# Two thirds of the modulation in 16 steps of 256 columns on four column tiles, not 32 steps of 512 columns on two

## The chip, the cores and the metric

The kernel runs on one core of a Trainium2 chip. The metric is the device time of one execution in microseconds; less is better. Times of before are the median of three runs, and the profile is of one execution.

## The reference

One decoder layer, for a prompt group of 1024 tokens and a sample group of 8 sequences with one new token each. Of it the change touches the modulation: a vector per sequence (8 of the sample group and one of the prompt, so 9) goes through `silu`, a matrix of 1024 x 6144 and a bias, and gives shift, scale and gate for the two halves of the layer.

```
mod = (jax.nn.silu(c) @ w_ada + b_ada)[:, None, :]
shift1, scale1, gate1, shift2, scale2, gate2 = jnp.split(mod, 6, axis=-1)
h = x * (1 + scale1) + shift1
qa, ka, va, rq, rk, rv, rg, ga, gb = jnp.split(h @ w_in, _in_splits(), axis=-1)
...
y_att = o_att.reshape(B, S, ATTN_OUT_WIDTH) @ w_att_out
y_ret = (jax.nn.silu(rg) * o_ret) @ w_ret_out
mixed = (jax.nn.sigmoid(ga) * y_att + jax.nn.sigmoid(gb) * y_ret) @ w_o
x = _layer_norm(DEEPNORM_ALPHA * x + gate1 * mixed, ln1_g, ln1_b)
h2 = x * (1 + scale2) + shift2
```

Only shift1 and scale1 (the first third, columns 0 to 2047) are needed before the input projection; gate1, shift2, scale2 and gate2 (the last two thirds) are first needed after `w_o`.

## The kernel before

Activations lie transposed in on-chip slots, 128 features by 1032 tokens each. A large product is done by `dense`: for one block of 128 output columns it goes over three chunks of 384, 384 and 264 tokens, and in each chunk `mm3` issues three matmuls for every block of 128 inputs (value and remainder: high x high, high x low, low x high), lines 191 to 193, into one bank `ps_d`. With 8 input blocks a dense is 72 matmuls, with 2 it is 18. Weights come through `wload`: a DMA from the SP queue into `w_raw` (line 174), a cast to `w_hi` on ScalarE (line 154) and a subtraction to `w_lo` on VectorE (line 155), each in a ring of three buffers, so a weight is cast when the dense three before it has ended.

The first third of the modulation is made at the start, by `prep`, eight times: 256 columns, all eight input blocks, in two loads of four blocks. The last two thirds are made by the generator `ada_rest`, which is advanced inside the loops over the gates. The gate loop A has eight rounds: a dense of 8 blocks for `ga` (called GA here) with a sigmoid on ScalarE as its evacuation (line 813), then a dense of 2 blocks for the attention output (called ATT) with a multiplication on VectorE (line 816). The gate loop G has eight rounds of one dense of 8 blocks (GB, sigmoid at line 827).

A matmul of the modulation (line 224, `ada_mm`) has the 9 vectors, padded to 32, as its stationary operand `cs`. Input block k writes the 32 PSUM partitions of column tile k modulo 4, and the four partial sums are added afterwards: `ada_finish` copies the bank to `m` on ScalarE (line 208), transposes it by blocks of 128 columns on TensorE (line 211), sums the four partial sums with a reduction on VectorE (line 214) and adds the bias (line 218). The loads `ada_raw` (line 232) and the copies `m` take slots from a first-in, first-out list of 40; in the last round of loop A 36 of them are held (16 by `hT`, 8 by `gated`, 4 by `oa`, 8 by `A`), and 4 go round.

Instructions stand on each engine in the order that the framework's scheduler gives them, so a transpose can stand some matmuls behind the step that it belongs to. An engine takes its instructions in that order.

Of the kernel before, what the change touches and what calls it, by code (L numbers as in the profile page):

```python
# [33 lines left out]
C_QA, C_KA, C_VA, C_RQ, C_RK, C_RV, C_RG, C_GA, C_GB = (  # L34
    0, 768, 1536, 2304, 2816, 3328, 4352, 5376, 6400)
# [69 lines left out]
def tile_hybrid_decoder_step(ctx: ExitStack, tc: tile.TileContext, a, o):  # L105
    nc = tc.nc
    dma_w = nc.sync
# [9 lines left out]
    slots = Slots()  # L117
    slots.add(slot_pool, N_SLOTS, "s")

    def bank(tag, shape, bufs):  # L120
        full = psum.tile([128, 512], F32, tag=tag, name="ps_" + tag, bufs=bufs)
        rows, inner = shape[0], shape[1:]
        n = int(np.prod(inner))
        ap = full[:rows, :n]
        if len(inner) == 2:
            ap = ap.rearrange("p (a b) -> p a b", a=inner[0])
        elif len(inner) == 3:
            ap = ap.rearrange("p (a b c) -> p a b c", a=inner[0], b=inner[1])
        return ap

    def dbank(shape=(128, 512)):
        return bank("d", shape, 3)

    def abank(shape=(128, 512)):
        return bank("a", shape, 2)

    def bbank(shape=(128, 512)):
        return bank("b", shape, 2)
# [33 lines left out]
    def wload(src, shape, eng=nc.vector, with_raw=False):  # L172
        raw = stream.tile(list(shape), F32, tag="raw", name="w_raw")
        dma_w.dma_start(raw[:], src)
        hi = stream.tile(list(shape), F32R, tag="hi", name="w_hi")
        lo = stream.tile(list(shape), F32R, tag="lo", name="w_lo")
        split(raw[:], hi[:], lo[:], eng)
        if rolling[0]:
            roll(hi)
        return (hi, lo, raw) if with_raw else (hi, lo)  # L180

    def wcols(w, c0, nk=8, k0=0, eng=nc.vector):
        return wload(w[128 * k0:128 * (k0 + nk), c0:c0 + 128].rearrange("(k p) c -> p k c", p=128),
                     (128, nk, 128), eng)

    def mm3(ps, w, acts, t0, n, k0=0, first=True, last=True):
        whi, wlo = w
        nk = len(acts)
        for k, (xhi, xlo) in enumerate(acts):
            f, l = first and k == 0, last and k == nk - 1  # L190
            nc.tensor.matmul(ps, whi[:, k0 + k, :], xhi[:, t0:t0 + n], start=f, stop=False)  # L191
            nc.tensor.matmul(ps, whi[:, k0 + k, :], xlo[:, t0:t0 + n], start=False, stop=False)  # L192
            nc.tensor.matmul(ps, wlo[:, k0 + k, :], xhi[:, t0:t0 + n], start=False, stop=l)  # L193

    def dense(w, acts, evac, chunks=TCH, k0=0, between=None):
        for t0, n in chunks:
            ps = dbank((128, n))
            mm3(ps, w, acts, t0, n, k0)
            evac(t0, n, ps)
            if between:  # L200
                next(between, None)

    w_ada, w_in = a["w_ada"], a["w_in"]

    def ada_finish(ps, chunks):
        n = 128 * len(chunks)
        m = slots.alloc((128, n), name="m")
        nc.scalar.copy(m[:], ps)
        pt = bbank((128, len(chunks), 128))
        for j, c in enumerate(chunks):  # L210
            nc.tensor.transpose(pt[:, j, :], m[:, 128 * j:128 * j + 128], ident[:])
        for j, c in enumerate(chunks):
            parts = pt[:, j, :].rearrange("p (g r) -> p r g", g=4)
            nc.vector.tensor_reduce(modT[:, c, :], parts[:, 0:9, :], axis=AX.X, op=OP.add)
        c0, n = chunks[0], len(chunks)
        step = chunks[1] - c0
        mt = modT[:, c0:c0 + (n - 1) * step + 1:step, :]
        nc.vector.tensor_add(mt, mt, bT[:, c0:c0 + (n - 1) * step + 1:step].unsqueeze(2).to_broadcast([128, n, 9]))
        slots.free(m)

    def ada_mm(ps, k0, w):
        for k in range(w.shape[1]):
            g = (k0 + k) % 4
            nc.tensor.matmul(ps[32 * g:32 * g + 32], cs[:, k0 + k, :], w[:, k],  # L224
                             start=k0 + k < 4, stop=k0 + k >= 4)

    def ada_rest():
        for cg in range(4, 12):
            ps = abank((128, 512))
            for k0 in range(0, 8, 2):  # L230
                raw = slots.alloc((128, 2, 512), name="ada_raw")
                dma_w.dma_start(raw[:], w_ada[128 * k0:128 * k0 + 256, 512 * cg:512 * cg + 512]
                                .rearrange("(k p) c -> p k c", p=128))
                ada_mm(ps, k0, raw)
                slots.free(raw)
                if k0 == 6:
                    ada_finish(ps, range(4 * cg, 4 * cg + 4))
                yield

    rc, rs = slots.alloc(name="rope_c"), slots.alloc(name="rope_s")  # L240
    for t, v, r in ((rc, 1.0, 0), (rs, 0.0, 1)):
# [34 lines left out]
    hT = []  # L276
# [95 lines left out]
    for g, (win, dil) in enumerate(PATTERNS):  # L372
        ls = min(dil, 8)
        qk = []
        for c0 in (C_QA, C_KA):
            for p in range(2):
                dst = slots.alloc(name="qk")

                def evac(t0, n, ps, dst=dst):
                    sh = wk.tile([128, 384], F32, tag="sh", name="sh", bufs=2)  # L380
                    t1 = wk.tile([128, 384], F32, tag="t1", name="t1", bufs=2)
                    nc.vector.stream_shuffle(sh[:, :n], ps, shuf)
                    nc.vector.tensor_mul(t1[:, :n], ps, rc[:, t0:t0 + n])
                    nc.vector.tensor_mul(sh[:, :n], sh[:, :n], rs[:, t0:t0 + n])
                    m = min(n, S - t0)
                    if dil == 1:
                        nc.vector.tensor_add(dst[:, t0:t0 + n], t1[:, :n], sh[:, :n])
                    else:
                        ov = dst[:, :S].rearrange("p (r u) -> p u r", r=ls)[:, t0 // ls:(t0 + m) // ls, :]
                        nc.vector.tensor_add(ov, t1[:, :m].rearrange("p (u r) -> p u r", r=ls),  # L390
                                             sh[:, :m].rearrange("p (u r) -> p u r", r=ls))
                        if n > m:
                            nc.vector.tensor_add(dst[:, S:T], t1[:, m:n], sh[:, m:n])

                if g == 0 and c0 == C_QA:
                    for (t0, n), ps in zip(TCH, first_ps[p]):
                        evac(t0, n, ps)
                else:
                    dense(wcols(w_in, c0 + 256 * g + 128 * p), hT, evac)
                qk.append(dst)  # L400
# [29 lines left out]
        for bi in range(8):  # L430
# [6 lines left out]
            nk, k0 = 128 * len(kb), 128 * kb[0]  # L437
# [228 lines left out]
    for h in range(4):  # L666
# [3 lines left out]
        for c0 in (C_RQ, C_RK):  # L670
            dst = slots.alloc(name="rqk")

            def evac(t0, n, ps, dst=dst):
                sw = wk.tile([128, 384], F32, tag="sh", name="sw", bufs=2)
                t1 = wk.tile([128, 384], F32, tag="t1", name="t1", bufs=2)
                nc.scalar.copy(sw[0:64, :n], ps[64:128])
                nc.scalar.copy(sw[64:128, :n], ps[0:64])
                nc.vector.tensor_mul(t1[:, :n], ps, rc[:, t0:t0 + n])
                nc.vector.tensor_mul(sw[:, :n], sw[:, :n], rs[:, t0:t0 + n])
                nc.vector.tensor_add(dst[:, t0:t0 + n], t1[:, :n], sw[:, :n])  # L680

            dense(wcols(w_in, c0 + 128 * h), hT, evac)
            qk.append(dst)
# [117 lines left out]
    oa = []  # L801
    for p in range(2):
# [3 lines left out]
        oa.append((hi, lo))  # L806
    A, G = [], []
    ada = ada_rest()
    for f in range(8):
        A.append(slots.alloc(name="A"))  # L810

        def sig(t0, n, ps, dst=A[f]):
            nc.scalar.activation(dst[:, t0:t0 + n], ps, AF.Sigmoid)

        def mul(t0, n, ps, dst=A[f]):
            nc.vector.tensor_mul(dst[:, t0:t0 + n], dst[:, t0:t0 + n], ps)

        dense(wcols(w_in, C_GA + 128 * f), hT, sig, between=ada)
        dense(wcols(a["w_att_out"], 128 * f, nk=2), oa, mul)
    rolling[0] = True  # L820
    for hi, lo in oa:
        slots.free(hi, lo)
    for f in range(8):
        G.append(slots.alloc(name="G"))

        def sig(t0, n, ps, dst=G[f]):
            nc.scalar.activation(dst[:, t0:t0 + n], ps, AF.Sigmoid)

        dense(wcols(w_in, C_GB + 128 * f), hT, sig, between=ada if f < 4 else None)
    for hi, lo in hT:  # L830
        slots.free(hi, lo)
    gs = [(slots.alloc(dtype=F32R, name="g_hi"), slots.alloc(dtype=F32R, name="g_lo")) for _ in range(8)]
# [63 lines left out]
    for t0, n in TLAST:  # L896
        gm = [slots.alloc((128, 2, 512), name="gm") for _ in range(4)]
        m = min(n, S - t0)
        for f in range(8):
            ps = dbank((128, n))  # L900
# [6 lines left out]
        for tb, rows in blks:  # L907
            x = slots.alloc((128, D), name="x1")
            dma_o.dma_start(x[:rows], a["x_prompt"][tb:tb + rows] if tb < S else a["x_sample"])
            for half in range(2):  # L910
                pz = abank((rows, 512))
                for j in range(4):
                    f = 4 * half + j
# [8 lines left out]
            for half in range(2):  # L922
                pb = bbank((128, 4, rows))
                for j in range(4):
                    f = 4 * half + j
# [3 lines left out]
                if tb < S:  # L929
                    for j in range(4):  # L930
                        f = 4 * half + j
# [9 lines left out]
                for j in range(4):  # L941
                    f = 4 * half + j
# [118 lines left out]
    for ci, (t0, n) in enumerate(TLAST):  # L1061
# [8 lines left out]
        for part in range(parts):  # L1070
            fs = range(step * part, step * part + step)
            for i, f in enumerate(fs):
                ps = dbank((128, n))
# [64 lines left out]
```

## Time and profile before

| what | value |
|---|---|
| median of 3 runs | 1970.76 us (1969.75 to 1972.15) |
| span of the profiled execution, first to last instruction | 1970.4 us |
| TensorE busy | 1924.3 us, 98% of the span |
| weight loads on TensorE | 1815.7 us, 92% |
| VectorE, ScalarE, GpSimd busy | 40%, 28%, 12% |
| loops A and G with the first matmuls behind them, 746 to 1015 us | TensorE busy 269.00 of 269.00 us, clock 1.00 |

The page gives no other time for the profiled execution than its span, which is 0.36 us under the median. Busy time of TensorE is modelled (matmuls overlap), so the rows below are read by the starts of neighbouring matmuls, not by their durations. A row of the time line gives the start, the busy time, the engine, the line, the operation with output and inputs, the shapes, and how many instructions are merged in it. A matmul in 32-bit floating point, as line 224's, stands in the trace as two instructions ("records"): the 64 matmuls of before are 128 records.

### The profile page before, as it was taken

To read this page: it belongs to the slowest core of one execution; us is meant where nothing else is said; L and a number is where in the kernel's file an instruction comes from. 1 tells how busy PE (TensorE), PEld (TensorE's weight loads), DVE (VectorE), ACT (ScalarE), POOL (GpSimd) and SP (SyncE) were. 2 spreads that over 40 slices of the span, in tenths; PEclk is the share of its full clock that TensorE was granted. 3 is DMA by queue.
4 is the path that set the end of the run, shared out by engine and by line. 5 is a ranking of instruction groups with operands and counts; after the bars stand their busy time and mean duration, and the time that the engine had idled before them with its cause. 6 is when DMAs were issued, how large, how long until landed. Compare 5 with 4: busy or idle time off the path is not lost.

```text
span 1970.4 us, 29739 instructions
## 1 busy us (share of the span) xinstructions
PE 1924.3 (98%) x12406; PEld 1815.7 (92%) x12406; DVE 793.9 (40%) x1824; ACT 550.9 (28%) x1118; POOL 229.3 (12%) x310
## 2 busy tenths in 40 slices
PE   7999999999999999999999999999999999999996
PEld 5879979889998998888999989999999999999996
DVE  4736153377644341211165366221133323323338
ACT  3251140424243342112132454212221112111212
POOL 2000000032000000000001553000000000000015
PEclk9999999999999999999999999999999999999998
DMA  9301101185223143334211554223343534444332
GB/s 273 105 25 33 50 26 44 55 238 166 76 68 100 56 134 106 112 113 129 63 56 56 173 169 137 76 75 109 110 166 129 183 128 154 139 137 139 107 108 86
DMA packets 209080, 217.21 MB, mean 110 GB/s; under 512 B 7621, under 2 KB 185133, under 8 KB 208178
## 3 DMA queue, kind: packets, MB, share of 16 engines
q1 hardware_dynamic: 190962, 117.50, 20.8%
q0 software_dynamic: 17856, 97.72, 13.9%
q8 instruction: 97, 1.59, 0.3%
q14 instruction: 37, 0.30, 0.0%
q10 hardware_dynamic: 128, 0.10, 0.0%
HBM read 193.88 MB, written 65.45 MB: 132 GB/s over the span
## 4 chain that ended last, share of the span: by engine, by line
PE 85%; issue 4%; DVE 4%; DMA 3%; ACT 2%; POOL 1%; SPq 1%; DVEq 0%; POOLq 0%; ACTq 0%
PE ps_d L191 22%; PE ps_d L192 22%; PE ps_d L193 22%; PE ps_d L357 3%; PE ps_d L359 3%; PE ps_d L358 3%; PE ps_a L224 2%; PE ps_a L444 1%; DMA qb<-dq 1%; PE ps_b L462 1%; PE ps_o L471 1%; POOL w_lo L155 1%; DMA vb<-dv 1%; DVE h_lo L155 1%; DMA wb<-dw 1%
## 5 line engine op out<-in xcount | busy, mean ns | idle before, releaser
L191 PE MATMUL ps_d<-h_hi,w_hi 128*128 128x384 f32 (+3 forms) x2064 | 667.1, 323 | 0.6 <-ACT tm L1015 0.6
L192 PE MATMUL ps_d<-h_lo,w_hi 128*128 128x384 f32 (+3 forms) x2064 | 663.5, 321 | 0.0
L193 PE MATMUL ps_d<-h_hi,w_lo 128*128 128x384 f32 (+3 forms) x2064 | 662.2, 321 | 0.0
L191 PEld LDWEIGHTS ps_d<-h_hi,w_hi 128*128 128x128 f32 x2064 | 388.3, 188 | 23.7 <-issue 17.6
L193 PEld LDWEIGHTS ps_d<-h_hi,w_lo 128*128 128x128 f32 x2064 | 388.3, 188 | 2.8 <-issue 2.3
L192 PEld LDWEIGHTS ps_d<-h_lo,w_hi 128*128 128x128 f32 x2064 | 388.3, 188 | 2.6 <-issue 1.8
L155 DVE TENSOR_TENSOR w_lo<-w_raw,w_hi 128x1024 fp32r<-128x1024 f32 (+2 forms) x140 | 158.4, 1132 | 387.2 <-ACT w_hi L154 386.5
L154 ACT CAST w_hi<-w_raw 128x1024 fp32r<-128x1024 f32 (+2 forms) x164 | 161.7, 988 | 471.9 <-PE ps_d L192 397.6
L1018 DVE TENSOR_TENSOR tm<-tm,ps_d 128x392 f32<-128x392 f32 (+2 forms) x66 | 33.9, 513 | 272.0 <-PE ps_d L193 270.5
L357 PE MATMUL ps_d<-w_hi,h_hi 128*128 128x256 f32 x448 | 141.6, 316 | 0.0
L359 PE MATMUL ps_d<-w_lo,h_hi 128*128 128x256 f32 x448 | 140.9, 315 | 0.7 <-DVE w_lo L155 0.7
L358 PE MATMUL ps_d<-w_hi,h_lo 128*128 128x256 f32 x448 | 140.8, 314 | 0.0
L191 PE MATMUL ps_d<-ff_hi,w_hi 128*128 128x384 f32 (+1 forms) x432 | 138.3, 320 | 0.0
L193 PE MATMUL ps_d<-ff_hi,w_lo 128*128 128x384 f32 (+1 forms) x432 | 138.1, 320 | 0.0
L192 PE MATMUL ps_d<-ff_lo,w_hi 128*128 128x384 f32 (+1 forms) x432 | 138.1, 320 | 0.0
L357 PEld LDWEIGHTS ps_d<-w_hi,h_hi 128*128 128x128 f32 x448 | 102.9, 230 | 3.0 <-issue 2.6
L359 PEld LDWEIGHTS ps_d<-w_lo,h_hi 128*128 128x128 f32 x448 | 103.0, 230 | 0.9 <-DVE w_lo L155 0.9
L358 PEld LDWEIGHTS ps_d<-w_hi,h_lo 128*128 128x128 f32 x448 | 103.1, 230 | 0.0
L168 POOL COPY tick<-tk 1x1 f32<-1x1 f32 x54 | 10.9, 202 | 706.3 <-DVE tk L167 706.3
L154 ACT CAST ff_hi<-tm 128x392 fp32r<-128x392 f32 (+2 forms) x66 | 31.6, 479 | 187.8 <-DVE tm L1018 187.8
L191 PEld LDWEIGHTS ps_d<-ff_hi,w_hi 128*128 128x128 f32 x432 | 81.2, 188 | 0.0
L192 PEld LDWEIGHTS ps_d<-ff_lo,w_hi 128*128 128x128 f32 x432 | 81.1, 188 | 0.0
(324 smaller groups left out, 2722.0 us busy)
## 6 DMA issues: line engine op xcount, KB each, us to landing
w_raw<-w_in SPq DMA_DIRECT2D x56, 512.0 KB, 4.3
w_raw<-w_ffn_in SPq DMA_DIRECT2D x44, 512.0 KB, 3.9
ada_raw<-w_ada SPq DMA_DIRECT2D x32, 512.0 KB, 4.2
sample_k<-cache_k POOLq DMA_DIRECT2D x8, 2047.0 KB, 10.2
sample_v<-cache_v POOLq DMA_DIRECT2D x8, 2047.0 KB, 9.3
w_raw<-w_o SPq DMA_DIRECT2D x24, 512.0 KB, 3.8
w_raw<-w_ffn_out SPq DMA_DIRECT2D x24, 384.0 KB, 3.4
ada_raw<-w_ada SPq DMA_DIRECT2D x32, 256.0 KB, 5.7
```

The source lines that it names most:

```text
L154: nc.scalar.copy(hi, raw)
L155: eng.tensor_sub(lo, raw, hi.bitcast(F32))
L191: nc.tensor.matmul(ps, whi[:, k0 + k, :], xhi[:, t0:t0 + n], start=f, stop=False)
L192: nc.tensor.matmul(ps, whi[:, k0 + k, :], xlo[:, t0:t0 + n], start=False, stop=False)
L193: nc.tensor.matmul(ps, wlo[:, k0 + k, :], xhi[:, t0:t0 + n], start=False, stop=l)
L224: nc.tensor.matmul(ps[32 * g:32 * g + 32], cs[:, k0 + k, :], w[:, k], start=k0 + k < 4, stop=k0 + k >= 4)
L357: nc.tensor.matmul(ps[:, j, :], xh, whi, start=k == 0, stop=False)
L358: nc.tensor.matmul(ps[:, j, :], xl, whi, start=False, stop=False)
L359: nc.tensor.matmul(ps[:, j, :], xh, wlo, start=False, stop=k == 7)
L444: nc.tensor.matmul(sb[hh][:, p, :nk], qT[p][r, 128 * bi:128 * bi + 128], kT[p][r, k0:k0 + nk], start=True, stop=True)
L462: nc.tensor.transpose(pb[:, j, :], pm[h][:, 128 * b:128 * b + 128], ident[:])
L1018: nc.vector.tensor_mul(tm[:, :n], tm[:, :n], pu)
```

## The change

`ada_rest` goes over 16 groups of 256 columns, not 8 groups of 512. A step loads all eight input blocks of a group (two loads of 512 KB, as large as the loads of before), issues eight matmuls of 256 columns on the four column tiles, two for each tile, and ends the group. Before, a step was one load and two matmuls of 512 columns, on two of the column tiles, and every fourth step ended a group. `dense` advances the generator once at its end, not after each of its three chunks; loop A advances it after GA and after ATT, and loop G no longer.

```
         for t0, n in chunks:
             ps = dbank((128, n))
             mm3(ps, w, acts, t0, n, k0)
             evac(t0, n, ps)
-            if between:
-                next(between, None)
+        if between:
+            next(between, None)
...
     def ada_rest():
-        for cg in range(4, 12):
-            ps = abank((128, 512))
-            for k0 in range(0, 8, 2):
-                raw = slots.alloc((128, 2, 512), name="ada_raw")
-                dma_w.dma_start(raw[:], w_ada[128 * k0:128 * k0 + 256, 512 * cg:512 * cg + 512]
+        for cg in range(8, 24):
+            ps = abank((128, 256))
+            raws = [slots.alloc((128, 4, 256), name="ada_raw") for _ in range(2)]
+            for kh, raw in enumerate(raws):
+                dma_w.dma_start(raw[:], w_ada[512 * kh:512 * kh + 512, 256 * cg:256 * cg + 256]
                                 .rearrange("(k p) c -> p k c", p=128))
-                ada_mm(ps, k0, raw)
-                slots.free(raw)
-                if k0 == 6:
-                    ada_finish(ps, range(4 * cg, 4 * cg + 4))
-                yield
+            for kh, raw in enumerate(raws):
+                ada_mm(ps, 4 * kh, raw)
+            slots.free(*raws)
+            ada_finish(ps, range(2 * cg, 2 * cg + 2))
+            yield
...
         dense(wcols(w_in, C_GA + 128 * f), hT, sig, between=ada)
-        dense(wcols(a["w_att_out"], 128 * f, nk=2), oa, mul)
+        dense(wcols(a["w_att_out"], 128 * f, nk=2), oa, mul, between=ada)
...
-        dense(wcols(w_in, C_GB + 128 * f), hT, sig, between=ada if f < 4 else None)
+        dense(wcols(w_in, C_GB + 128 * f), hT, sig)
```

On TensorE, at the end of the first GA, where ATT's matmuls (inputs `oa`) begin; a row with x4 is four matmuls:

```order
 L192 MATMUL ps_d<-h_lo_619,w_hi 128x264
 L193 MATMUL ps_d<-h_hi_618,w_lo 128x264
-L224 MATMUL ps_a<-ada_raw_7213,cs 32x512 x2
+L224 MATMUL ps_a<-ada_raw_7205,cs 32x256 x4
+L224 MATMUL ps_a<-ada_raw_7206,cs 32x256 x4
 L191 MATMUL ps_d<-oa_hi_7111,w_hi 128x384
 L192 MATMUL ps_d<-oa_lo_7112,w_hi 128x384
 L193 MATMUL ps_d<-oa_hi_7111,w_lo 128x384
+L211 MATMUL ps_b<-ident,m_7217 128x128 x2
 L191 MATMUL ps_d<-oa_hi_7115,w_hi 128x384
 L192 MATMUL ps_d<-oa_lo_7116,w_hi 128x384
```

The third step of before is now the first step of the new form, with its two transposes three matmuls behind it; the steps after the first and second chunk of GA are gone. Before, the four transposes of a group stood six matmuls behind its fourth step.

On ScalarE, from the end of the first GA to the second; `A` is the sigmoid of a chunk, `m` the copy of a group, and the cast of 1024 columns that of the weight two rounds on:

```order
 L813 ACTIVATE A_7119<-ps_d 128x264
-L154 CAST w_hi<-w_raw 128x1024
-L813 ACTIVATE A_7247<-ps_d 128x384
-L208 COPY m_7284<-ps_a 128x512
-L813 ACTIVATE A_7247<-ps_d 128x384
+L208 COPY m_7217<-ps_a 128x256
+L154 CAST w_hi<-w_raw 128x1024
+L208 COPY m_7268<-ps_a 128x256
+L813 ACTIVATE A_7276<-ps_d 128x384 x2
 L154 CAST w_hi<-w_raw 128x256
```

Each round of loop A now has two copies of 256 columns, the second of them directly behind the cast of 1024 columns; before, a copy of 512 columns stood between or behind sigmoids.

On the SP queue of the changed kernel, the loads of the last two steps (`ada_raw_234` and `ada_raw_235` of the fifteenth, `ada_raw_237` and `ada_raw_238` of the sixteenth) and of weights for loop G:

```order
L232 DMA ada_raw_234_8304<-w_ada 128x4x256
L232 DMA ada_raw_235_8305<-w_ada 128x4x256
L232 DMA ada_raw_237_8355<-w_ada 128x4x256
L174 DMA w_raw_8643<-w_in 128x8x128
L232 DMA ada_raw_238_8356<-w_ada 128x4x256
L174 DMA w_raw_8732<-w_in 128x8x128
```

By the list of slots `ada_raw_238` takes the slot of `ada_raw_234`, one step before it, with only ATT between the two; `ada_raw_235` takes one of the step before it too, with GA between; every other load takes one last used at least two steps before. Behind loop G the order on all engines is that of before.

## Rows read from the trace of the kernel before

**Rows 1.** The page's head and its part 1: span; busy time, share, instructions.

```profile
span 1970.4 us, 29739 instructions
PE 1924.3 (98%) x12406; PEld 1815.7 (92%) x12406; DVE 793.9 (40%) x1824; ACT 550.9 (28%) x1118; POOL 229.3 (12%) x310
```

**Rows 2.** One stretch: length, busy by engine, granted clock, DMA share, GB/s.

```profile
746.00:1015.00 269.00, 269.00 (x1613) 235.26 (x1612) 63.51 (x145) 62.14 (x115) 9.18 (x24) 1.00 0.33 101
```

**Rows 3.** Time line of TensorE, first chunk of loop A and its step.

```profile
746.27 0.34 PE L191 MATMUL ps_d<-h_hi,w_hi 128*128 128x384 f32 x1
...
750.29 0.33 PE L193 MATMUL ps_d<-h_hi,w_lo 128*128 128x384 f32 x1
750.55 1.05 PE L224 MATMUL ps_a<-ada_raw,cs 128*32 128x512 f32 x4
751.53 0.44 PE L191 MATMUL ps_d<-h_hi,w_hi 128*128 128x384 f32 x1
751.81 0.34 PE L192 MATMUL ps_d<-h_lo,w_hi 128*128 128x384 f32 x1
```

**Rows 4.** Time line of TensorE: a chunk of 264 tokens; the first matmul behind loop G.

```profile
757.12 0.28 PE L192 MATMUL ps_d<-h_lo,w_hi 128*128 128x264 f32 x1
...
759.82 0.28 PE L193 MATMUL ps_d<-h_hi,w_lo 128*128 128x264 f32 x1
...
990.89 0.34 PE L191 MATMUL ps_d<-g_hi,w_hi 128*128 128x384 f32 x1
```

**Rows 5.** Time line of all engines behind the fourth step: copy and transposes.

```profile
769.20 0.44 PE L191 MATMUL ps_d<-h_hi,w_hi 128*128 128x384 f32 x1
...
769.32 0.59 ACT L208 COPY m<-ps_a 128x512 f32<-128x512 f32 x1 [0.50 <-PE ps_a L224]
...
770.18 0.34 PE L193 MATMUL ps_d<-h_hi,w_lo 128*128 128x384 f32 x1
...
770.35 0.60 PE L211 MATMUL ps_b<-ident,m 128*128 128x128 f32 x4
...
770.97 0.34 PE L192 MATMUL ps_d<-h_lo,w_hi 128*128 128x384 f32 x1
```

**Rows 6.** Time line of TensorE, last round of the first third (`prep`).

```profile
54.51 0.29 PE L286 MATMUL ps_o<-h_hi,wf_lo 128*128 128x264 f32 x1
54.73 1.07 PE L224 MATMUL ps_b<-ada_raw,cs 128*32 128x256 f32 x16
55.73 0.66 PE L313 MATMUL ps_b<-ident,x 128*128 128x128 f32 x4
...
57.90 0.43 PE L285 MATMUL ps_d<-h_lo,wf_hi 128*128 128x384 f32 x1
58.16 0.38 PE L211 MATMUL ps_b<-ident,m 128*128 128x128 f32 x2
...
58.56 0.34 PE L284 MATMUL ps_d<-h_hi,wf_hi 128*128 128x384 f32 x1
```

**Rows 7.** Copies of 256 columns, ns min/median/max; time line at ATT's end.

```profile
L208 ACT COPY m<-ps_b x8: 366/372/375, 15.1 to 57.1; 128x256 f32<-128x256 f32 x8
...
763.82 0.28 PE L193 MATMUL ps_d<-oa_hi,w_lo 128*128 128x264 f32 x1
...
764.02 1.05 ACT L154 CAST w_hi<-w_raw 128x1024 fp32r<-128x1024 f32 x1 [3.31 <-PE ps_d L192]
```

**Rows 8.** Tile `ada_raw`: weight loads of 32 columns, landing; loads 860 to 935 us.

```profile
L224 PEld LDWEIGHTS ps_a<-ada_raw,cs x128: 106/108/109, 750.5 to 930.0; 128*32 128x32 f32 x128
...
DMA to landing us min/median/max: 3.7/4.2/6.2
...
ada_raw<-w_ada SPq DMA_DIRECT2D x10, 512.0 KB, 5.4
```

**Rows 9.** Waits: who for whom, us in total, times, longest.

```profile
PEld ps_a L224 <- issue: 5.1, 21, 0.2
...
SPq L232 <- PE ps_a L224: 73.5, 15, 8.5
```

## Prediction

> **What bounds the kernel now.** I read the page's head and its table of engines first: TensorE is busy 98% of the span, no other engine over 40% [rows 1]. That is an average, so I took the stretch that holds loops A and G by itself: TensorE is busy for all of it, at a granted clock of 1.00, the upper of its two levels, 2.4 GHz, while DMA moves 101 GB/s at a third of its share [rows 2]. The table of waits then says that the modulation's matmuls waited for nothing but "issue", 0.2 us at a time [rows 9]: no load was late for a step. So in this stretch the end is set by the sum of what stands on TensorE, and anything taken off that queue comes off the time, unless a wait takes its place.
>
> Busy time doesn't price a step, since matmuls overlap; starts do. In a chunk of 384 tokens 24 matmuls start within 23 pitches from 746.27 to 750.29, so the pitch is 4.02 / 23 = 0.175 us [rows 3]; in a chunk of 264 it is (759.82 - 757.12) / 22 = 0.123 us [rows 4].
>
> One step of before: the last dense matmul ahead starts at 750.29, the second one behind at 751.81. That is 1.52 us where two pitches would take 0.35, so a step takes 1.17 us off TensorE [rows 3]. It has three parts: 0.09 us beyond the pitch before line 224 starts, 0.98 us of line 224, and 0.10 us by which the first matmul of the full array behind it is slower than its pitch. Four transposes of a group: from 770.18 to 770.97 are 0.79 us in place of 0.35, so 0.44 us [rows 5].
>
> The prices can be checked against the stretch. Loops A and G hold 16 dense of 8 blocks (48 x 0.175 + 24 x 0.123 = 11.34 us) and 8 of 2 blocks (2.83 us): 204.0 us. With 32 x 1.17 + 8 x 0.44 = 41.0 us that makes 245.0 us. From 746.27 [rows 3] to the first matmul behind loop G at 990.89 [rows 4] are 244.6 us. There is no other loss in it to be had.
>
> **The change part by part.** *Removed:* 32 steps and 8 groups of four transposes, 41.0 us of TensorE.
>
> *Added, the matmuls.* The new step, eight blocks of 256 columns on four column tiles, already runs in this trace, in the first third: 16 records start at 54.73 behind a dense matmul at 54.51, and the next instruction starts at 55.73 [rows 6]. That is 1.22 us less a pitch of 0.123, so 1.10, and with the 0.10 for the first full-array matmul behind it 1.20 us. So a new step costs TensorE what an old one costs (1.20 against 1.17) and does twice the work: 16 x 1.20 = 19.2 us. Below, it can't be cheaper than the old step by any row (16 x 1.17 = 18.7). I take 19.2.
>
> The row says 16 records of 256 columns cost 1.00 us where 4 of 512 cost 0.98 [rows 3, 6]: four times as many instructions are hidden in the overlap. The Trainium skill (TensorEngine Tiling (Array Packing), section Instruction Overhead) says that each matmul carries about 60 cycles of overhead; for the 128 records more than before that would be, as an estimate from that page at 2.4 GHz, 128 x 25 ns = 3.2 us, and the gain 3.2 us less. The trace doesn't show such a cost in this form, so the sum goes by the rows.
>
> *Added, the transposes.* As many as before, but in 16 pairs. A pair costs 58.56 - 57.90 - 0.35 = 0.31 us [rows 6]: 16 x 0.31 = 5.0 us. By halving the 0.44 of four it would be 3.5, the lower bound.
>
> *Added waits, TensorE for ScalarE.* The pair now stands only three dense matmuls behind its step, where the four stood six. Call D the start of the first dense matmul behind a step. A copy begins at D + 0.12 [rows 5], takes 0.37 us for 256 columns [rows 7], so ends at D + 0.49. The third matmul behind starts at about D + 0.10 + 2 x 0.175 = D + 0.45, and the weight load of the transposes could go then, as it did at 770.18. With some 0.05 us from the copy's end to TensorE that is a wait of near 0.1 us. What is queued behind it on TensorE is everything, so it counts: 16 x 0.08 = 1.3 us. The bounds are 0 (a copy that is in time) and 0.3 each, 4.8 us.
>
> At the end of ATT the copy stands behind the cast of 1024 columns. That cast began 0.20 us after ATT's last matmul started and takes 1.05 [rows 7]; it would end at +1.25. Line 224 ends 0.07 us behind D, and D is 0.20 + 1.00 = +1.20 there. So the copy, due at +1.3, finds ScalarE just free. It costs nothing if the cast starts as it did; the margin is under 0.1 us, and a rival below prices its loss.
>
> *Moved, the loads.* Still 32 of 512 KB, so as many bytes and issues on the SP queue; landing 4.2 us in the median, 6.2 at most [rows 8]. Loads of SP waited for slots freed by line 224, 73.5 us in total [rows 9], without TensorE noticing. A load is needed at its step, and its slot, but for one, is freed at least a GA (11.3 us) before: covered. Weight loads behind them on SP are issued two dense and more ahead, so a block of a few us there reaches nobody. The exception is the last load: its slot is freed when the first half of the fifteenth step ends. From there to the need are 0.5 us of that step, 0.31 of its transposes, 2.83 of ATT, and 0.2 + 0.5 until the sixteenth step's second half, 4.4 us in all. With the landing of 5.4 us that loads had late in the stretch [rows 8] it is 1.0 us late, once. Bounds: 0 (4.2) and 1.8 (6.2).
>
> *Moved, VectorE and ScalarE.* Eight more additions and copies in pieces: some 1 us on engines that are idle for more than half of these 269 us [rows 2], off the path. Loop G loses its steps and stays bound by TensorE. Behind it every engine's order is as before, so I count nothing there.
>
> **Sum.** -41.0 + 19.2 + 5.0 + 1.3 + 1.0 = -14.5 us. The span of 1970.4 becomes 1955.9; with the 0.36 us by which the median of the runs lies above that span, 1956.3 us, 0.7% less. The cheapest ends (18.7 + 3.5, no wait) give -18.8, 1952.0; the dearest (19.2 + 5.0 + 4.8 + 1.8) give -10.2, 1960.6.
>
> **Rivals.** *The finish comes twice as often, and TensorE waits there.* If the copies behind ATT don't find ScalarE free, each of the eight waits up to a whole cast: 8 x 1.05 = 8.4 us, and the time is 1956.3 + 8.4 = 1964.7. For it speaks the thin margin above and that TensorE has nothing else to take; against it, that the cast starts as soon as ATT's matmuls release its buffer [rows 7], before line 224 has begun. Still faster than before.
>
> *The added instructions are paid for.* The change would then not do what it says. If each of the 128 added records cost one weight load of 32 columns (0.108 us [rows 8]), 13.8 us come back: 1970.1, no change. Against it stands the step of the first third, 1.00 us for 16 records [rows 6], with other inputs the same instruction for instruction.
>
> *Loads come late at every step behind ATT, and the kernel is slower.* There a step has only ATT between itself and the one before, and it now needs two loads, not one. If the slots made each of these loads wait for the step before, as the last one does, eight steps would wait by the landing less 4.4 us. At the 6.2 us of the slowest load [rows 8] that is 1.8 x 8 = 14.4 us, less the 1.0 already counted: 1969.7, the gain gone. It decides for slower (over 1974.7) from 2.4 us each, a landing of 6.8, as could come from loads queued behind each other: 8 x 2.5 = 20 us gives 1975.3. Against it: by the list of slots only the last load is so placed, and before no step waited for a load [rows 9].
>
> **Chances.** A measurement of this kernel tells from no change what is over 0.2%, 3.9 us. My forecast with its bounds, 1952.0 to 1960.6: 0.85. Waits at the finish, 1961 to 1966: 0.08. Paid-for instructions, and the weaker form of late loads, within 0.2%: 0.04. Late loads to the full: 0.03. The first two are faster, 0.93; same 0.04; slower 0.03. The predicted time is 1956.3. The forecast's own bounds nearly hold the 8 in 10; I widen them by about half a us on either side, since the waits at the finish are worked out from margins of tenths: 1951.5 to 1961.0.
>
> **What would show it.** In the profile after: 256 records of line 224 from loops A and G (now 128), 16 in about 1.00 us from their first start to the next dense matmul; steps right if the distance of the dense matmuls around one is 1.5 us, wrong if 2 or more. Pairs of transposes 0.3 to 0.4 us; TensorE's waits for `m`, about 0.1 us each, in the table of waits for line 211, and one wait of about 1 us for `ada_raw` ahead of the last step. From the first matmul of loop A to the first behind loop G 230 us, where it was 244.6; the stretches ahead and behind as long as before. The prediction is wrong if line 224 waits for loads at more steps than the last, if line 211 waits for casts, or if a stretch behind loop G changes its length by more than 2 us though its order is the same.

## The result and the profile after

The changed kernel takes 1953.56 us, the median of four runs (1952.79 to 1954.22); the kernel before, in the same rounds, 1971.45 us (four runs, 1969.75 to 1973.21). The ratio is 0.9907, interval 0.9894 to 0.9919: a gain of 17.9 us, where 14.5 were forecast. The time lies inside the forecast's own bounds and nearer their cheap end.

The page's head and its part 1 of the changed kernel, to be put beside [rows 1]:

```profile
span 1952.4 us, 30025 instructions
PE 1905.2 (98%) x12534; PEld 1817.5 (93%) x12534; DVE 794.4 (41%) x1832; ACT 551.8 (28%) x1126; POOL 229.2 (12%) x310
```

There are 128 records more on TensorE, and TensorE is still busy for 98% of the span, 19.1 us less of it. Where the time went is seen by cutting the span at the first matmul of loop A and at the first one behind loop G. The three stretches of the changed kernel (start and end, length, busy by engine, granted clock, DMA share, GB/s):

```profile
0.00:747.91 747.91, 720.71 (x4829) 651.97 (x4830) 366.13 (x971) 258.91 (x574) 74.25 (x116) 1.00 0.33 94
747.91:974.09 226.18, 226.18 (x1587) 213.01 (x1585) 45.41 (x111) 50.34 (x95) 6.67 (x20) 1.00 0.39 119
974.09:1952.40 978.31, 958.27 (x6123) 952.49 (x6121) 382.89 (x751) 242.60 (x458) 148.25 (x174) 0.99 0.37 123
```

and the middle one of the kernel before:

```profile
746.27:990.89 244.62, 244.62 (x1458) 210.88 (x1457) 44.05 (x103) 49.14 (x87) 6.71 (x20) 1.00 0.34 105
```

The loops fell from 244.62 to 226.18 us, by 18.44, with TensorE busy for all of them at a granted clock of 1.00, as before. The stretch ahead is 1.64 us longer (746.27 to 747.91) and the one behind 1.20 us shorter (979.51 to 978.31), though TensorE, VectorE, ScalarE and GpSimd have the same order there. In each, one wait far from the change moves by more than the difference. From the table of waits (who for whom, us in total, times, longest), of the kernel before:

```profile
PE ps_b L701 <- ACT kt L707: 3.6, 2, 3.2
PE ps_a L1083 <- DVE acc L958: 2.7, 1, 2.7
```

and of the changed kernel:

```profile
PE ps_b L701 <- ACT kt L707: 6.4, 2, 6.0
PE ps_a L1083 <- DVE acc L958: 1.2, 1, 1.2
```

So -18.44 + 1.64 - 1.20 = -18.0 us, which is the difference of the spans. That these two waits set the lengths of their stretches is not shown: among the experiments below, one starts loop A at 748.32 with a wait of 3.8 us at line 701's place, and one has a stretch behind the loops of 977.67 us with the 2.7 us of before.

The first new step, on the time line of the changed kernel (all engines, rows of TensorE, its weight loads and ScalarE's copy kept):

```profile
759.08 0.28 PE L193 MATMUL ps_d<-h_hi,w_lo 128*128 128x264 f32 x1
759.29 1.07 PE L224 MATMUL ps_a<-ada_raw,cs 128*32 128x256 f32 x16
760.29 0.44 PE L191 MATMUL ps_d<-oa_hi,w_hi 128*128 128x384 f32 x1
760.43 0.37 ACT L208 COPY m<-ps_a 128x256 f32<-128x256 f32 x1 [0.45 <-PE ps_a L224]
760.58 0.34 PE L192 MATMUL ps_d<-oa_lo,w_hi 128*128 128x384 f32 x1
760.75 0.34 PE L193 MATMUL ps_d<-oa_hi,w_lo 128*128 128x384 f32 x1
760.85 0.21 PEld L211 LDWEIGHTS ps_b<-ident,m 128*128 128x128 f32 x2
760.92 0.38 PE L211 MATMUL ps_b<-ident,m 128*128 128x128 f32 x2
761.06 0.42 PE L191 MATMUL ps_d<-oa_hi,w_hi 128*128 128x384 f32 x1
761.32 0.34 PE L192 MATMUL ps_d<-oa_lo,w_hi 128*128 128x384 f32 x1
```

Sixteen records take 1.00 us (759.29 to 760.29). From 759.08 to 760.58 are 1.50 us in place of a pitch of 0.123 and one of 0.175: the step costs 1.20 us, the number that [rows 6] had given. The pair of transposes costs less than forecast: 760.75 to 761.32 are 0.57 us in place of 0.35, so 0.22. The copy ends at 760.80 and the transposes' weight load goes 0.05 us behind it, at 760.85. That is 0.10 us later than on the pitch (the weight load for 760.75 went at 760.58), but still 0.07 us ahead of its matmul, which starts at 760.92, one pitch behind the one before it. So TensorE's matmuls don't wait for this copy.

In four of the sixteen steps the copy ends 0.05 us later behind its step, and its weight load goes only 0.01 to 0.02 us ahead of the matmul. There the pair costs 0.27 us (0.62 in place of 0.35 in the first of them), 0.2 us more in all:

```profile
794.67 0.33 PE L193 MATMUL ps_d<-oa_hi,w_lo 128*128 128x384 f32 x1
...
795.29 0.34 PE L192 MATMUL ps_d<-oa_lo,w_hi 128*128 128x384 f32 x1
```

The second step of the round, at the end of ATT, where the margin to the cast was thin:

```profile
763.33 0.28 PE L193 MATMUL ps_d<-oa_hi,w_lo 128*128 128x264 f32 x1
763.53 1.04 ACT L154 CAST w_hi<-w_raw 128x1024 fp32r<-128x1024 f32 x1 [2.72 <-PE ps_d L192]
...
764.54 0.45 PE L191 MATMUL ps_d<-h_hi,w_hi 128*128 128x384 f32 x1
...
764.68 0.37 ACT L208 COPY m<-ps_a 128x256 f32<-128x256 f32 x1
...
765.00 0.34 PE L193 MATMUL ps_d<-h_hi,w_lo 128*128 128x384 f32 x1
...
765.18 0.38 PE L211 MATMUL ps_b<-ident,m 128*128 128x128 f32 x2
```

The cast ends at 764.57, the copy starts at 764.68, 0.14 us behind the step's first dense matmul (D, 764.54), as it does behind GA, and the transposes are on their pitch again (765.00, 765.18). In all eight rounds this cast ends 0.03 us behind D, ahead of the copy. The table of waits of this stretch has no row of line 211 for `m`, and none of line 224 for a load. The last load, which was to be 1.0 us late:

```profile
878.90 0.37 SPq L232 DMA_DIRECT2D ada_raw<-w_ada  x1
...
882.24 0.28 PE L193 MATMUL ps_d<-oa_hi,w_lo 128*128 128x264 f32 x1
882.45 1.07 PE L224 MATMUL ps_a<-ada_raw,cs 128*32 128x256 f32 x16
883.45 0.45 PE L191 MATMUL ps_d<-h_hi,w_hi 128*128 128x384 f32 x1
```

It was issued at 878.90; its half of the step is due 0.5 us behind 882.45, and the burst is not longer than the others (1.00 us). So it landed within about 4.1 us; the loads whose landing the trace gives took 3.6 to 6.6 us, 4.6 in the median. In a second trace of this kernel the last load, issued at 880.13 and 4.0 us ahead of its need, was in time again.

### The profile page after: what moved, and what is told of

It reads as the page before. It is cut to its first block, busy times and chain, and to the rows that moved or that the text cites. A ratio compares the mean times of both kernels' runs of the same rounds, so it can differ in the third digit from the quotient of the medians.

```text
span 1952.4 us, 30025 instructions
## 1 busy us (share of the span) xinstructions
PE 1905.2 (98%) x12534; PEld 1817.5 (93%) x12534; DVE 794.4 (41%) x1832; ACT 551.8 (28%) x1126; POOL 229.2 (12%) x310
## 4 chain that ended last, share of the span: by engine, by line
PE 88%; DVE 3%; DMA 3%; ACT 2%; issue 2%; POOL 1%; SPq 1%; DVEq 0%; POOLq 0%; ACTq 0%
PE ps_d L191 23%; PE ps_d L192 23%; PE ps_d L193 23%; PE ps_d L357 3%; PE ps_d L359 3%; PE ps_d L358 3%; DMA w_raw<-w_in 2%; PE ps_a L444 2%; PE ps_b L462 1%; PE ps_o L471 1%; PE ps_a L224 1%; POOL w_lo L155 1%; DMA vb<-dv 1%; DVE h_lo L155 1%; PE ps_o L719 1%
## 5 line engine op out<-in xcount | busy, mean ns | idle before, releaser
L193 PEld LDWEIGHTS ps_d<-ff_hi,w_lo 128*128 128x128 f32 x432 | 81.1, 188 | 0.0
```

## The experiments

The theory: loops A and G are the sum of TensorE's queue, a new step costs 1.20 us because sixteen records of 256 columns on four column tiles take hardly longer than four of 512 on two (1.00 against 0.98), and a pair of transposes costs 0.22. The rivals, each with an experiment: the number of steps, of instructions or the place of the steps makes the gain, not the column tiles; the finish is near to a wait; the slots are near to a wait. As a measure of all of them serves the length of the loops (first matmul of loop A to first matmul behind loop G) less that of the first experiment, which has no modulation in them.

**Without the modulation's last two thirds.** It leaves out the products of the last two thirds; their values are the bias alone.

```
     def ada_rest():
-        for cg in range(8, 24):
...
-            ada_finish(ps, range(2 * cg, 2 * cg + 2))
-            yield
+        nc.vector.tensor_copy(modT[:, 16:48, :], bT[:, 16:48].unsqueeze(2).to_broadcast([128, 32, 9]))
+        yield
```

> The last two thirds of the modulation are left out (no loads, matmuls, copies or transposes; modT there is the bias alone). Theory (everything of it stands on TensorE and nothing else is bound to it): the changed kernel loses 16 steps of 1.20 us and 16 pairs of transposes of 0.22 us, 22.7 us, and the time is 1953.6 - 22.7 = 1930.9 us, within 1.5 us. Rival (the loads or the steps also disturb other work, or part of the steps was hidden): a difference other than 22.7 us by more than 3 us, and a change in the length of a stretch outside loops A and G.

Measured: 1933.13 us (four runs, 1928.47 to 1934.65), 0.9801 of before (0.9788 to 0.9814). Its loops:

```profile
747.78:951.35 203.57, 203.57 (x1298) 203.46 (x1297) 38.49 (x63) 44.56 (x79) 6.67 (x20) 1.00 0.19 57
```

203.57 us, where the pitches had given 204.0. So the modulation cost the loops 244.62 - 203.57 = 41.05 us before (41.0 were worked out) and costs 226.18 - 203.57 = 22.61 now; 16 x (1.20 + 0.22) = 22.7. So those two prices account for it, and these 22.6 us are all that the modulation still costs in the loops. The time fell by 20.4 us, not by the 22.7 that were expected: the stretch behind the loops is 979.45 us here, 1.14 more than in the changed kernel's trace, and its four runs spread over 6.2 us.

**Two column tiles in the new step.** The same 16 steps, loads and places, but the eight blocks go to two column tiles, four to each; the finish sums two partial sums, so the transposes take 64 rows.

```
...
-                ada_mm(ps, 4 * kh, raw)
+                for k in range(4):
+                    g = k % 2
+                    nc.tensor.matmul(ps[32 * g:32 * g + 32], cs[:, 4 * kh + k, :], raw[:, k],
+                                     start=4 * kh + k < 2, stop=4 * kh + k >= 6)
             slots.free(*raws)
-            ada_finish(ps, range(2 * cg, 2 * cg + 2))
+            ada_finish(ps[0:64], range(2 * cg, 2 * cg + 2), 64)
```

> 16 steps of 256 columns at the same places, but the eight blocks on two column tiles, not four (copies and transposes then have 64 rows). Theory (the gain comes from four column tiles at work instead of two): line 224 takes about 0.14 + 8 x 0.213 = 1.85 us a step, not 1.00, so 16 x 0.85 = 13.6 us come back: about 1967 us. Rival (only the number of steps counts, each with a fixed price): as the changed kernel, 1953.6 us.

Measured: 1969.78 us (11 runs, 1966.88 to 1973.07), 0.9987 of before (0.9978 to 0.9995). The time line of TensorE, first step:

```profile
757.49 0.28 PE L193 MATMUL ps_d<-h_hi,w_lo 128*128 128x264 f32 x1
757.70 1.92 PE L237 MATMUL ps_a<-ada_raw,cs 128*32 128x256 f32 x16
759.55 0.44 PE L191 MATMUL ps_d<-oa_hi,w_hi 128*128 128x384 f32 x1
...
760.00 0.34 PE L193 MATMUL ps_d<-oa_hi,w_lo 128*128 128x384 f32 x1
760.26 0.33 PE L211 MATMUL ps_b<-ident,m 64*128 64x64 f32 x2
760.52 0.44 PE L191 MATMUL ps_d<-oa_hi,w_hi 128*128 128x384 f32 x1
760.81 0.33 PE L192 MATMUL ps_d<-oa_lo,w_hi 128*128 128x384 f32 x1
```

The burst is 1.85 us (757.70 to 759.55) where four tiles take 1.00, with as many instructions of the same size. The loops are 243.30 us, 39.73 for the modulation: 17.1 of the 18.4 us are gone. Part of that is an effect of the experiment itself: its pairs of transposes cost 0.46 us (760.00 to 760.81 in place of 0.35) and not 0.22. Without that it would be 35.9 us, an estimate. So of the 18.4 us, the two column tiles more bring 35.9 - 22.6 = 13.3, and 16 steps in place of 32 by themselves 41.05 - 35.9 = about 5.1. The column tiles make the larger part of the gain, not all of it.

**Half steps.** 32 steps at the places of before (after each chunk), each with one load and four blocks of 256 columns on the four tiles; every second one ends a group.

```
-        if between:
-            next(between, None)
+            if between:
+                next(between, None)
...
-            raws = [slots.alloc((128, 4, 256), name="ada_raw") for _ in range(2)]
-            for kh, raw in enumerate(raws):
+            for kh in range(2):
+                raw = slots.alloc((128, 4, 256), name="ada_raw")
...
                 ada_mm(ps, 4 * kh, raw)
-            slots.free(*raws)
-            ada_finish(ps, range(2 * cg, 2 * cg + 2))
-            yield
+                slots.free(raw)
+                if kh:
+                    ada_finish(ps, range(2 * cg, 2 * cg + 2))
+                yield
...
-        dense(wcols(a["w_att_out"], 128 * f, nk=2), oa, mul, between=ada)
+        dense(wcols(a["w_att_out"], 128 * f, nk=2), oa, mul)
...
-        dense(wcols(w_in, C_GB + 128 * f), hT, sig)
+        dense(wcols(w_in, C_GB + 128 * f), hT, sig, between=ada if f < 4 else None)
```

> The change in half: 256 columns on four column tiles, but four blocks a step, so 32 steps, one after each chunk of 384 or 264 as before. Theory (a step has a fixed part of 0.20 us beside it and about 0.14 in it, the rest goes with columns over four tiles): 32 x (0.20 + 0.14 + 0.43) + 16 x 0.22 = 28.2 us in place of 22.7, so 5.4 us slower than the changed kernel: about 1959 us. Rival (a step costs 1.2 us whatever is in it): 32 x 1.20, 19 us slower: about 1973 us.

Measured: 1958.75 us (five runs, 1956.21 to 1960.32), 0.9934 (0.9921 to 0.9947); loops 231.79, modulation 28.22. Time line of TensorE, a step:

```profile
750.95 0.33 PE L193 MATMUL ps_d<-h_hi,w_lo 128*128 128x384 f32 x1
751.21 0.64 PE L224 MATMUL ps_a<-ada_raw,cs 128*32 128x256 f32 x8
751.78 0.44 PE L191 MATMUL ps_d<-h_hi,w_hi 128*128 128x384 f32 x1
752.06 0.34 PE L192 MATMUL ps_d<-h_lo,w_hi 128*128 128x384 f32 x1
```

The step is 1.11 - 0.35 = 0.76 us, its burst 0.57: half the work of 1.00 costs more than half of it. Sixteen steps more cost 28.22 - 22.61 = 5.61 us, 0.35 each. By the rows the fixed part of a step is 0.33: 0.09 of entry, 0.10 for the first matmul of the full array behind it, and 2 x 0.57 - 1.00 = 0.14 inside the burst. This divides the gain from the other side, and alike: four column tiles with the 32 steps of before bring 41.05 - 28.22 = 12.8 us, and 16 steps in place of 32 the other 5.6.

**Two fixed slots.** All 32 loads go through the same two slots, so every step's loads wait for the step before it; this tests the rival of the late loads.

```
+        raws = [slots.alloc((128, 4, 256), name="ada_raw") for _ in range(2)]
         for cg in range(8, 24):
             ps = abank((128, 256))
-            raws = [slots.alloc((128, 4, 256), name="ada_raw") for _ in range(2)]
...
-            slots.free(*raws)
+            if cg == 23:
+                slots.free(*raws)
```

> The changed kernel, with its 32 loads of the modulation bound to the same two slots, so that each load waits for the step before. Theory (loads cost nothing as long as a whole GA lies between slot and need, and cost their lateness where only ATT does): the eight steps behind ATT wait 0.5 to 1.5 us each, 4 to 12 us, so 1958 to 1966 us, and the steps behind GA wait for nothing. Rival (loads are hidden behind ATT too, as the last load of the changed kernel was): 1953.6 us.

Measured: 1958.62 us (six runs, 1955.11 to 1963.63), 0.9935 (0.9921 to 0.9948); loops 232.13, modulation 28.56, 5.95 more than in the changed kernel. Waits of this kernel in the loops:

```profile
PEld ps_a L224 <- PE ps_d L193: 3.7, 7, 0.9
...
PE ps_a L224 <- DMA ada_raw<-w_ada: 2.6, 7, 0.7
```

and the first step behind an ATT, on the time line of TensorE:

```profile
763.73 0.28 PE L193 MATMUL ps_d<-oa_hi,w_lo 128*128 128x264 f32 x1
764.29 0.64 PE L224 MATMUL ps_a<-ada_raw,cs 128*32 128x256 f32 x8 [0.27 <-DMA ada_raw<-w_ada]
...
766.10 0.64 PE L224 MATMUL ps_a<-ada_raw,cs 128*32 128x256 f32 x8
```

Only the steps behind ATT wait, as the rival had it; those behind GA don't. At 764.29 the wait is 0.35 us (0.56 behind 763.73, where 0.21 is usual). But the experiment did a second thing: the scheduler put six dense matmuls between the halves of these steps, so each pays the fixed part once more. Read in the same way, the eight waits are 0.21 to 0.78 us, 3.3 in all, and eight second entries at 0.33 are 2.6: 5.9 of the 5.95 us. The waits had been expected at 0.5 to 1.5 us each. Loads landed in 4.5 us in the median, 5.2 at most. So the mechanism exists, its price is tenths of a us for a step with the loads of this kernel, and the slots of the changed kernel keep clear of it.

**Eight steps of 512 columns.** Eight blocks of 512 columns on four tiles, behind GA alone; four loads of (128, 2, 512).

```
-        for cg in range(8, 24):
-            ps = abank((128, 256))
-            raws = [slots.alloc((128, 4, 256), name="ada_raw") for _ in range(2)]
+        for cg in range(4, 12):
+            ps = abank((128, 512))
+            raws = [slots.alloc((128, 2, 512), name="ada_raw") for _ in range(4)]
...
-            ada_finish(ps, range(2 * cg, 2 * cg + 2))
+            ada_finish(ps, range(4 * cg, 4 * cg + 4))
...
-        dense(wcols(a["w_att_out"], 128 * f, nk=2), oa, mul, between=ada)
+        dense(wcols(a["w_att_out"], 128 * f, nk=2), oa, mul)
```

> One step further: 8 steps of 512 columns by all eight blocks on four column tiles, one behind each GA. Theory (a step is 0.20 us beside it, 0.14 in it, and its columns over four tiles): 8 x (0.20 + 0.14 + 1.71) + 8 x 0.44 for transposes in fours = 19.9 us of TensorE where the changed kernel has 22.6, so 2.7 us less: about 1951 us, and loops A and G take 223.5 us from first matmul to the first behind them. Rival (the four loads of a step, in slots that the step before used, come late): waits for loads in the table of waits, and no gain.

Measured: 1952.2 us (five runs, 1949.91 to 1954.99), 0.9899 (0.9881 to 0.9917); loops 223.65, modulation 20.08. Time line of TensorE, a step:

```profile
757.05 0.28 PE L193 MATMUL ps_d<-h_hi,w_lo 128*128 128x264 f32 x1
757.26 1.92 PE L224 MATMUL ps_a<-ada_raw,cs 128*32 128x512 f32 x16
759.11 0.44 PE L191 MATMUL ps_d<-oa_hi,w_hi 128*128 128x384 f32 x1
759.39 0.34 PE L192 MATMUL ps_d<-oa_lo,w_hi 128*128 128x384 f32 x1
```

The burst of twice the columns is 1.85 us, not 2.00: the 0.14 inside the burst is paid once. The loops are 2.53 us shorter than those of the changed kernel, which the prices give: the steps are 2.7 us less (8 x 2.05 against 16 x 1.19), the transposes 0.2 more (3.96 us in all against 3.74). The fours cost 0.50 here and 0.44 in the kernel before; the table of waits has their weight loads behind the longer copy four times. The rival of late loads doesn't come: each step starts 0.21 us behind the dense matmul ahead (757.05 to 757.26), as in the changed kernel.

**Sixteen steps of 512 columns by four blocks.** The changed kernel's 16 places and loads, but half as many matmuls of twice the columns; every second step ends a group of 512.

```
-        for cg in range(8, 24):
-            ps = abank((128, 256))
...
+        for cg in range(4, 12):
+            ps = abank((128, 512))
+            for kh in range(2):
+                raws = [slots.alloc((128, 2, 512), name="ada_raw") for _ in range(2)]
...
+                    ada_mm(ps, 4 * kh + 2 * q, raw)
+                slots.free(*raws)
+                if kh:
+                    ada_finish(ps, range(4 * cg, 4 * cg + 4))
+                yield
```

> 16 steps at the places of the changed kernel, but each 512 columns by four blocks on four column tiles (half the matmuls, each twice as long, groups ended every second step, transposes in fours). Theory (columns over four tiles decide, not how many instructions they are in): 16 x 1.20 + 8 x 0.44 = 22.7 us of TensorE, the same as the changed kernel, 1953.6 us. Rival (each matmul has a price of its own, which the halving of their number saves): up to 128 records x 0.025 to 0.108 us less, 3 to 14 us faster.

Measured: 1954.71 us (five runs, 1953.25 to 1955.64), 0.9906 (0.989 to 0.9921); loops 226.26, modulation 22.69. Time line of TensorE:

```profile
757.56 0.28 PE L193 MATMUL ps_d<-h_hi,w_lo 128*128 128x264 f32 x1
757.77 1.06 PE L224 MATMUL ps_a<-ada_raw,cs 128*32 128x512 f32 x8
758.77 0.44 PE L191 MATMUL ps_d<-oa_hi,w_hi 128*128 128x384 f32 x1
```

Eight records of 512 columns take 1.00 us, as sixteen of 256. With four column tiles at work the number of instructions costs nothing that shows here, only the columns in each tile. The rival of the paid-for instructions falls: with 128 records less the sixteen steps took 19.0 us against 19.1, and the loops changed by 0.08 us.

**The copy done twice.** ScalarE copies `m` twice in each step, 0.41 us more ahead of the transposes.

```
         nc.scalar.copy(m[:], ps)
+        if n == 256 and chunks[0] > 15:
+            nc.scalar.copy(m[:], ps)
```

> The changed kernel with the copy of each group of the last two thirds done twice on ScalarE, so m is ready 0.37 us later. The scheduler then puts the pair of transposes five dense matmuls behind a step, not three. Theory (the scheduler puts the transposes where it expects m, so TensorE doesn't wait for the copy): 0 us, 1953.6. Rival of the prediction (the finish is at the edge, TensorE waits there as soon as the copy is later): 16 x 0.3 to 0.4 us, 5 to 6 us slower.

Measured: 1954.87 us (five runs, 1953.81 to 1955.44), 0.9907 (0.9892 to 0.9922); loops 226.64, modulation 23.07, 0.46 us more in all. Time line of ScalarE and TensorE, first step:

```profile
758.64 0.37 ACT L210 COPY m<-ps_a 128x256 f32<-128x256 f32 x1
...
758.90 0.33 PE L192 MATMUL ps_d<-oa_lo,w_hi 128*128 128x384 f32 x1
759.07 0.43 PE L213 MATMUL ps_b<-ident,m 128*128 128x128 f32 x2
...
759.52 0.34 PE L191 MATMUL ps_d<-oa_hi,w_hi 128*128 128x384 f32 x1
```

The experiment missed its aim: the scheduler placed the transposes five dense matmuls behind the step in place of three, so the copy was hardly late. It ends at 759.01, and the weight load goes at 759.06, 0.01 us ahead of its matmul. Fifteen of the sixteen pairs cost about 0.27 us (759.52 - 758.90 - 0.35), as the four late ones of the changed kernel do, 0.5 us in all. So the place of the transposes isn't fixed at three matmuls, and a copy that is late by this little costs 0.05 us; what a later one costs was not measured.

**The new steps after each chunk.** The changed kernel's steps at the places of before: all 16 in the first five and a third rounds, three behind each GA.

```
-        if between:
-            next(between, None)
+            if between:
+                next(between, None)
...
-        dense(wcols(a["w_att_out"], 128 * f, nk=2), oa, mul, between=ada)
+        dense(wcols(a["w_att_out"], 128 * f, nk=2), oa, mul)
```

> The new steps, one after each chunk of GA as before, so 16 steps in the first five and a third rounds of loop A. Theory (the form of the step brings the gain, not its place): line 224 and the transposes take the same 22.6 us, and the time is 1953.6 us but for loads that come late, since now six of 512 KB fall in each round: what these cost stands as waits for ada_raw. Rival (the place, a step at the end of a dense only, brings a part of the gain): the step's own distance grows from 1.50 us, or the stretch grows without waits for loads.

Measured: 1955.61 us (five runs, 1950.24 to 1955.66), 0.9905 (0.9887 to 0.9922); loops 226.68, modulation 23.11. A step there costs 1.54 - 0.35 = 1.19 us (750.72 to 752.26), and no load was late, though one took 8.7 us to land. So the place of the steps is worth half a us at most.

**The changed kernel and the eight steps again,** side by side, since their times lay close.

> The changed kernel once more, on the same chip as the next run, so that the two can be compared: 0.991 of the kernel before.

> The 8 steps of 512 columns by eight blocks once more, beside the changed kernel. Theory: 2.5 us less than the changed kernel, 0.13%, of which the first measurement showed 226.2 - 223.6 us in loops A and G. Rival: no difference, since four loads a step come late or cost elsewhere.

Measured: the changed kernel 1954.31 us (four runs, 1953.6 to 1955.82; 0.9902, 0.9886 to 0.9919), eight steps 1953.29 us (four runs, 1951.19 to 1955.28; 0.9898, 0.9883 to 0.9913). The loops are 226.16 and 223.68 us, so again 2.5 apart; the times of the runs don't tell the two apart. In both pairs of traces the loops of eight steps are shorter, but that this version is faster as a whole is not shown.

## Why the prediction was right, and where its sizes were off

**What bounds the stretch** was right: the loops are the sum of TensorE's queue, and what came off it came off the time. The experiment without the modulation gives the dense work at 203.57 us (204.0 worked out), and the removed work at 41.05 (41.0).

**The step at 1.20 us** was right to the hundredth, since the same burst stood in the trace already [rows 6]. The law behind it, from the bursts of all kernels, is a fixed 0.33 to 0.35 us for a step, 0.14 of it inside the burst, and then the columns that each tile takes: the burst is 0.57 us for two records of 256 a tile, 1.00 for four of 256 or two of 512 (0.98 for two of 512 on the two tiles of before), 1.85 for eight of 256 or four of 512.

**The pair of transposes** was mis-sized: 0.31 forecast, 0.22 measured, the lower bound; 16 times, 1.4 us. The row that it was read from [rows 6] starts at 57.90 with a duration of 0.43 us, not 0.34: a dense matmul that itself stands first behind other transposes, so its 0.10 us was put down to the pair. It should have been read from a pair that stands between matmuls on their pitch, or halved from the four of [rows 5].

**The waits for the copy** were mis-sized: 16 x 0.08 = 1.3 us forecast, 4 x 0.05 = 0.2 measured. The copy's end was forecast nearly rightly (D + 0.49; it was D + 0.51 in eleven steps, at ATT's end too, and up to D + 0.59 in the others), and so was the weight load, 0.10 us late. What failed is the step from a late weight load to a late matmul: a weight load usually goes 0.17 us ahead of its matmul, here 0.07, and the matmul starts on its pitch. Only where the lead shrank to 0.01 or 0.02 us did the pair take longer.

**The last load** was mis-sized too: 1.0 us late forecast, not late measured. The 4.4 us to its need were about right (878.90 to about 882.95 are 4.05 from the start of its issue), but it landed in that time, under the median of 4.6, and not in the 5.4 us taken for the late loads. Why it came faster than most is not shown; at the median it would have been half a us late.

These three make 1.4 + 1.1 + 1.0 = 3.5 us of the 3.9 by which the loops gained more than 14.5; the steps, at 1.19 to 1.20, left 0.1, and the rest is as small as the rounding of the pitches (204.0 worked out, 203.57 measured). **The stretches outside** were said to stay as long as before, the one behind within 2 us. They changed by +1.64 and -1.20. The kernels here, with the same order on TensorE ahead of loop A, start it between 745.72 and 749.14 (the changed kernel itself at 747.91 and 749.14), and their stretches behind the loops take 977.67 to 979.64 us, so this is spread of executions.

**The rivals.** The finish that waits for the cast didn't come: the cast starts 0.20 us behind ATT's last matmul, and the copy found ScalarE free by 0.11 us or more in all eight rounds. Paid-for instructions are excluded by the kernel with half of them. The Trainium skill (TensorEngine Tiling (Array Packing), section Instruction Overhead) gives each matmul about 60 cycles of overhead. By that, as a cost added to each record, the 128 records that this kernel saves would be worth, as an estimate from that page at 2.4 GHz, 3.2 us; the loops measured 226.26 against 226.18 us, so the trace doesn't agree for matmuls that overlap on column tiles. Late loads at each step behind ATT need slots that make each step wait for the last; forced to that, the kernel lost 5.95 us, about half of it by waits, and stayed faster than before.

## What to carry to other kernels

When the stationary operand is narrow, use all four column tiles in every step before thinking of fewer or larger instructions: the same 16 records took 1.00 us on four tiles and 1.85 on two, and that was 13 of the 18 us. Then make few entries, which was the other 5: each time that TensorE left the full array and came back cost some 0.35 us beside the columns, in half steps as in whole ones. And read a small price only where both neighbours are on their pitch: a neighbour that still pays for another switch puts its 0.1 us on the wrong account.

## What the runs showed of the hardware that was not expected

Transposes with 64 rows cost twice those with 128: 0.46 us a pair against 0.22, though each transposes half as many elements (64 x 128 in place of 128 x 128). The cause is open. The starts show 0.09 us more ahead of them and 0.12 us more within the pair; the copy is not what they wait for, since in the first step it ends at 760.02 and the weight load goes at 760.26. That a smaller tile of the array has to be entered, as by the modulation's matmuls, would fit the first of these, but was not tested apart.

One wait ahead of the loops, of line 701 for ScalarE's `kt`, took 3.6 us in one execution and 6.4 and 7.4 in two of another kernel with the same order of instructions on the engines. The start of loop A moves by 3.4 us between kernels with that order ahead of it, more than the 2.5 us by which the eight steps are shorter. This wait doesn't explain it alone (3.8 us where loop A starts at 748.32, 3.6 where it starts at 746.27); the cause is open.
